# A hybrid SSD, attention and mLSTM step on one core: the rows of decays loaded on SP's queue by the part ahead, an mLSTM tile of their own, one bias buffer

## The chip, the core and the metric

The kernel runs on 1 core of one Trainium2 chip. The metric is the device time of one execution in microseconds (us); lower is better. A core has a matrix engine (TensorE, PE in the profile; PEld is its weight load), VectorE (DVE), ScalarE (ACT), GpSimd (POOL) and SyncE (SP), and 16 DMA engines that move data between the chip's DRAM and the on-chip memory. Each engine runs its own instructions in the order in which they were queued. SP computes nothing here; its queue issues transfers. ScalarE and POOL issue some too, out of the same queue as their computing.

## The reference

One step of one layer of a streaming encoder, for 512 prompt frames and 64 sample frames (T = 576 columns): `x + 1/2 SwiGLU(RMSNorm(x))`, then `+ Mixer(RMSNorm(x))`, then `+ 1/2 SwiGLU(RMSNorm(x))`, and a last RMSNorm. The mixer projects its input once and feeds three branches:

- SSD (Mamba-2): 16 heads of 64 in 4 groups, chunked scan. With `cum = cumsum(dt * a)` the weights inside a chunk are `exp(cum[t] - cum[s])`, and the state enters with `exp(cum)`.
- band attention: 8 heads of 64, with a learned bias on clipped relative distance.
- mLSTM: 4 heads of 128 with exponential gates. With `m` the running maximum of the log weights, a chunk uses `exp(logd - m)` and the state enters with `ei = exp(inter - m)`.

```python
seg = cum[:, :, None] - cum[:, None, :]
lmat = jnp.exp(jnp.where(causal, seg, -jnp.inf))
y = jnp.einsum('btsgr,bsgrp->btgrp', w, xc) + jnp.exp(cum)[..., None] * jnp.einsum('btgn,bgrpn->btgrp', cc, h)
...
s = jnp.einsum('bthd,bshd->btsh', qc, kc) * jnp.exp(logd - mt[:, :, None])
num = jnp.einsum('btsh,bshd->bthd', s, vc) + ei[..., None] * jnp.einsum('bthk,bhkv->bthv', qc, c)
```

Each branch is projected, gated and summed. So the SSD needs, for each of its 16 heads, a row of `cum` over all 576 frames, and the mLSTM, for each of its 4 heads, a row of `-m` and one of `ei`. These are the rows of decays that this case is about.

## The kernel before

All of it is float32, with each operand of a matmul split into a high and a low part (three matmuls a product; the helper at L288 and L289 makes the parts, ScalarE the high one, VectorE the low one). Features lie on the 128 partitions, frames along the free axis. Weights come through rings of buffers: `wr`, `wx` and `wy` for what is loaded, `ph` and `pl` for the parts. SP's queue issues the weight loads (L237, L460, L467), POOL's one accumulating transfer a pair of blocks (L461). The big products (L616) use a scheme of seven products for eight blocks; `uv` (L533) and `g`, `P` (L540, L542) are where ScalarE and VectorE empty their accumulators.

The run has three stages: a first feed-forward part, the mixer, a second feed-forward part. In the mixer the projections are a stream of products. Ahead of every product, `tick` takes one step of a side job (`gates`, until it ends) and one step of the first job in a queue: `attn`, `ml` or `ssd` of one part. The parts come in the order a0 a1 m0 s0 a2 a3 s1 m1 s2 m2 s3 m3, where a is a pair of attention heads, m an mLSTM head and s an SSD group of four heads; an SSD group works in two halves `j` of two heads each. A job yields how many products are to pass until its next step. The program is written in this order, but the order on each engine is set when the kernel is built: the framework places instructions by their place in the program as priority, as soon as its own timing says that operands and buffers are there, and adds the waits. So an instruction with nothing to wait for can be placed far ahead of its part. Tiles of one tag share a number of buffers (`BUFS`), and a new tile waits until an older one of its tag has been read.

`gates` (L784 on) computes all the rows once, at the start of the mixer, from the projection `pre`: it turns `pre` to put frames on partitions (L794), works there, turns the result back, and stores 24 rows of 576 to a scratch tensor in DRAM, `scr_rows` (L839, L853, L856): 0 to 15 the SSD's `cum`, 16 to 19 the mLSTM's `-m`, 20 to 23 its `ei`. `rows` makes an access pattern that reads a row for many partitions, so a load spreads it.

`b` (L176) is the load: it issues, on ScalarE's queue (L181), one transfer of two spread rows, 576 KB, into two of the eight slots of `R1` (128 x 8 x 576, which holds x in the feed-forward parts). It takes slots 2 to 4 and 5 to 7 in turn, whoever calls it. `ml` calls it once at its start and gets `nmB` and `eiB`. `ssd` calls it at its start for both halves, and loads to the third slot of each the same two rows again, 64 partitions each (L1175, 144 KB a transfer). Slots 0 and 1 hold the SSD's gate z.

Readers of the rows. In `ml`: `qt` (POOL, L1045), the tile `D` of decays (VectorE, L1049; `D` is from the ring of four `P` tiles, which attention and the convolution use too), `wc` (ScalarE, L1067) and the state update (VectorE, L1083). In `ssd`, per half: `wd` (VectorE, L1209), `el` (ScalarE, L1212 and L1213), the decay matrices made in place from the first two slots (ScalarE, L1234 to L1237; POOL, L1238), read by matmuls at L1274, and the third slot, made `exp` in place (L1242), multiplied with the state's part (L1282) and added (L1284); the half ends with a product on POOL (L1287) and a store of `ys` on SP (L1288).

`attn` loads the bias table of its two heads at its start on ScalarE's queue (L916), subtracts a constant and masks it on POOL (L918 to L921), and reads it in the prompt's scores (L965) and, last, the sample's (L980, L981). The tag `bias` has two buffers.

Of the kernel before, what the change touches and what calls it, by code (L numbers as in the profile page):

```python
# [31 lines left out]
T = 576  # L32
# [4 lines left out]
NS = 115  # L37
FH = 288
NPLAIN = 4
BUFS = {"g": 9, "t": 5, "P": 4, "Q": 2, "bias": 2}  # L40

FBUFS = {"P": 5, "g": 5, "s": 3}
WBUFS = {"wr": 5, "wx": 4, "wy": 2, "ph": 6, "pl": 6}
# [38 lines left out]
class Hybrid:  # L82
    def __init__(self, ctx, tc, I, O):
        self.tc, self.nc, self.I, self.O = tc, tc.nc, I, O
        self.op = None
        self.stay = {}
        self.plan = []
        self.splan = []
        self.ahead = {}
        self.pin = {}  # L90
        self.b_i = 0
        self.jobs, self.gap, self.side = deque(), 0, iter(())
        nc = self.nc
        self.const = ctx.enter_context(tc.tile_pool(name="const", bufs=1))
        self.dram = ctx.enter_context(tc.tile_pool(name="scr", bufs=1, space=bass.MemoryType.DRAM))
        c = self.const
        self.R1 = c.tile([128, 8, T], F32, name="R1")
        self.rs = c.tile([128, T], F32, name="rs")
        self.small = ctx.enter_context(tc.tile_pool(name="small", bufs=8, reuse_waits="tile"))

        self.wt = ctx.enter_context(tc.tile_pool(name="wt", bufs=1, reuse_waits="tile"))
        self.xs = self.dram.tile([128, 8, T], F32, name="xs")

        self.ys = [self.dram.tile([128, T], F32, name=f"ys{i}") for i in range(16)]
        self.gs = [self.dram.tile([128, T], F32, name=f"gs{i}") for i in range(24)]
        self.scr = self.dram.tile([24, T], F32, name="scr_rows")
# [66 lines left out]
    def unit(self, shape, tag, bufs):  # L173
        return self.fp.tile(list(shape), F32, name=tag, tag=tag, bufs=bufs)

    def b(self, step, r0):  # L176


        i = 2 + self.b_i % 2 * 3
        self.b_i += 1  # L180
        self.nc.scalar.dma_start(self.R1[:, i:i + 2, :], self.rows(r0, 128, step))  # L181
        return [self.R1[:, i + j, :] for j in range(3)]

    def bank(self):
        i = self.bank_i % self.banks
# [598 lines left out]
    def gates(self, pre):  # L784
# [3 lines left out]
        nc, TM = self.nc, self.TM  # L788
        view = lambda i, w: self.R1[:, i, 0:5 * w].rearrange("p (c w) -> p c w", w=w)
        X, u, d, p, q = view(1, 24), view(2, 20), view(3, 20), view(4, 20), view(5, 20)  # L790
        nc.gpsimd.memset(X[64:128, 4, :], 0.0)
        ps = self.ps("x")
        for c, (a, n) in enumerate(CH):
            nc.tensor.transpose(ps[:n, c * 24:(c + 1) * 24], pre[0:24, a:a + n], self.ident[0:24, 0:24])  # L794
# [36 lines left out]
        RT, b, g, M, ei = (self.R1[:, i, :] for i in (6, 2, 3, 4, 5))  # L831
        ps, ps2 = self.ps("x"), self.ps("s")
        for c, (a, n) in enumerate(CH):
            o = ps[:, a:a + n] if c < 4 else ps2[:, 0:n]
# [32 lines left out]
            nc.tensor.transpose(ps[:n, c * 4:c * 4 + 4], b[0:4, a:a + n], self.ident[0:4, 0:4])  # L867
        nc.vector.tensor_copy(TM[:, 0:4, 96:100], ps[:, 0:16].rearrange("p (c w) -> p c w", w=4))
        nc.vector.tensor_copy(TM[:64, 4, 96:100], ps[:64, 16:20])

    def rows(self, r0, n, step=0):

# [159 lines left out]
    def ml(self, h, t):  # L1032
        nc = self.nc
        q, k, v, o = t["q"], t["k"], t["v"], t["o"]
        nmB, eiB, _ = self.b(4, 16 + h)
        C0 = self.unit([128, 130], "c0", 1)
        nc.scalar.dma_start(C0[:, :129], self.I["mc0"][h])
        kt, v1 = self.t("t", (128, 5, 128)), self.t("t", (128, 5, 129))
# [17 lines left out]
        s = self.ps("s")  # L1056
# [15 lines left out]
        for c, (a, n) in enumerate(CH):  # L1072
            if c == 4:
                C = C0
            wv = self.unit([128, 130], "wv", 2)
            nc.scalar.activation(wv[:n, :129], v1[:n, c, :], AF.Copy, scale=wc[:n, c:c + 1])
            pc = self.ps("s")
            nc.tensor.matmul(pc[:, :129], kt[:n, c, :], wv[:n, :129], start=True, stop=True)
            C2 = self.unit([128, 130], "cs", 4)
            if c == 0:  # L1080
                nc.vector.tensor_copy(C2[:, :129], pc[:, :129])
            else:
                nc.vector.scalar_tensor_tensor(C2[:, :129], C[:, :129], eiB[:, a + n - 1:a + n], pc[:, :129],  # L1083
                                               op0=ALU.mult, op1=ALU.add)
            b, o0 = where[c]
            ps = nums[b][:n, o0:o0 + 129]
            nc.tensor.matmul(ps, D[:n, a:a + n], v1[:n, c, :], start=True, stop=(c == 0))
            if c:
                nc.tensor.matmul(ps, qt[:, a:a + n], C[:, :129], start=False, stop=True)
            C = C2  # L1090
            if c >= 3:
                nc.sync.dma_start(self.O["c"][c - 3, h], C[:, :129])
            yield 1
        r = self.unit([128, 8], "r", 2)
        ss = self.unit([128, 8], "ss", 2)
# [2 lines left out]
        for c, (a, n) in enumerate(CH):  # L1098
            b, o0 = where[c]
# [3 lines left out]
        for c, (a, n) in enumerate(CH):  # L1103
            b, o0 = where[c]
# [6 lines left out]
        for c, (a, n) in enumerate(CH):  # L1111
            b, o0 = where[c]
# [55 lines left out]
    def ssd(self, g, t):  # L1168
        nc = self.nc
        Bf, Cf = t["B"], t["C"]  # L1170
        rows = []
        for j in range(2):
            rows.append(self.b(1, 4 * g + 2 * j))
            for r in range(2):
                nc.scalar.dma_start(rows[j][2][r * 64:(r + 1) * 64, :], self.rows(4 * g + 2 * j + r, 64))  # L1175

        last = nc.scalar.activation(self.R1[:, 0, :], self.R1[:, 0, :], AF.Silu)
        with self.tc.issue_after(last.ins):
# [20 lines left out]
        for j in range(2):  # L1199
# [30 lines left out]
            for r in range(2):  # L1230
                e = cum[r]
                tc_ = 32 + d0 + r
                for c, (a, n) in enumerate(CH):
                    nc.scalar.activation(e[:n, a:a + n], e[:n, a:a + n], AF.Relu, scale=-1.0,  # L1234
                                         bias=self.TM[:n, c, tc_:tc_ + 1])
# [10 lines left out]
            for c, (a, n) in enumerate(CH):  # L1246
# [9 lines left out]
                else:  # L1256
                    h = states[c]
# [11 lines left out]
            for c, (a, n) in enumerate(CH):  # L1269
                if c == 4:  # L1270
                    ps = self.ps("s")
                for r in range(2):
                    o = py[r * 64:(r + 1) * 64, a:a + n] if c < 4 else ps[r * 64:(r + 1) * 64, 0:64]
# [13 lines left out]
            nc.gpsimd.tensor_tensor(R[:, 512:], x[:, 515:], R[:, 512:], op=ALU.mult)  # L1287
            nc.sync.dma_start(self.ys[8 + 2 * g + j], R)  # L1288
            yield 1
        yield 3  # L1290

        for j in range(2):
# [316 lines left out]
```

## Time and profile before

| | |
|---|---|
| time, median of 3 runs | 1942.54 us (1939.22 to 1944.31) |
| time of the profiled execution | 1944.79 us |
| its span, first to last instruction | 1943.1 us |
| granted TensorE clock, mean | 0.991 |
| DMA, mean over the span | 152 GB/s |
| rows of 576 KB from `scr_rows`, ScalarE's queue | 12 |
| rows of 144 KB from `scr_rows`, ScalarE's queue | 16 |
| first and last issue of rows | 663.3 and 1145.0 us |

How to read the profile's lines: times are us from the start of the span. A line of a timeline has start, duration, engine, source line, operation, out<-in by tile names, shapes and count; in brackets the idle time of the engine before it and what ended it. An engine with a q is its queue issuing a transfer. A line of waits has who waited, for whom, us in total, times, and the longest. A line of windows has the stretch, then busy us (and instructions) of PE, PEld, DVE, ACT and POOL, then the granted TensorE clock as a share of full speed, the DMA engines' busy share and GB/s. A line of one source line or tile has the durations in ns (least, median, most), then first and last start. A line of DMA issues has tiles, queue, count, KB each and the median us from issue to landing.

### The profile page before, as it was taken

The numbers are of one execution on the slowest core, as the hardware profiler recorded it, in microseconds if no ns is written. First come the engines' busy times: TensorE is split into PE (matmuls) and PEld (weight loads), VectorE is DVE, ScalarE is ACT, GpSimd is POOL, SyncE is SP. The second block draws the span as 40 slices with busy tenths as digits, with TensorE's granted clock in tenths as the row PEclk, the third lists the DMA queues.
The fourth block names the chain that finished last, engine by engine and source line by source line (L and its number), as shares of the span: only waits on it lengthen the run. The fifth ranks groups of instructions, "written<-read, shape, count | busy, mean of one in ns | idle before, by whom it ended". The sixth has DMA issues, their size and how long they took to land. (4 is left out here: it accounts for less than half of the span.)

```text
span 1943.1 us, 37678 instructions
## 1 busy us (share of the span) xinstructions
PE 1887.2 (97%) x13901; PEld 1823.6 (94%) x13901; DVE 1524.6 (78%) x2715; ACT 1089.5 (56%) x2486; POOL 680.1 (35%) x656
## 2 busy tenths in 40 slices
PE   9999999999999999999999998999999999999998
PEld 8899999999999878888888888999999999999998
DVE  8998998988768767667777775745898888988865
ACT  4554654655544777767675765324555455554544
POOL 5343333333202234323435353440233334334311
PEclk9999999999999999899999999999999999999999
DMA  7267666666742545753667557742236666666631
GB/s 241 74 160 173 159 163 163 159 172 163 185 131 80 156 117 159 200 147 108 183 165 183 155 152 213 241 143 88 77 99 165 163 157 172 166 157 167 159 94 60
DMA packets 129440, 294.69 MB, mean 152 GB/s; under 512 B 14289, under 2 KB 26193, under 8 KB 129257
## 3 DMA queue, kind: packets, MB, share of 16 engines
q1 hardware_dynamic: 100072, 205.67, 32.7%
q0 software_dynamic: 19696, 72.10, 20.5%
q10 hardware_dynamic: 9488, 14.53, 2.6%
q8 instruction: 109, 1.79, 0.4%
q14 instruction: 75, 0.61, 0.1%
HBM read 272.87 MB, written 19.38 MB: 150 GB/s over the span
## 5 line engine op out<-in xcount | busy, mean ns | idle before, releaser
L616 PE MATMUL acc<-TH,ph 128*128 128x288 f32 x3220 | 968.0, 301 | 27.4 <-ACT uv L533 11.8
L616 PE MATMUL acc<-TL,ph 128*128 128x288 f32 x3220 | 955.4, 297 | 0.6 <-DVE TL L289 0.6
L616 PE MATMUL acc<-TH,pl 128*128 128x288 f32 x3220 | 955.0, 298 | 1.0 <-DVE pl L289 0.9
L616 PEld LDWEIGHTS acc<-TH,ph 128*128 128x128 f32 x3220 | 607.5, 189 | 46.9 <-ACT uv L533 15.5
L616 PEld LDWEIGHTS acc<-TL,ph 128*128 128x128 f32 x3220 | 609.4, 189 | 4.9 <-issue 3.7
L616 PEld LDWEIGHTS acc<-TH,pl 128*128 128x128 f32 x3220 | 608.4, 189 | 4.8 <-DVE pl L289 2.2
L289 DVE TENSOR_TENSOR pl<-wr,ph 128x512 fp32r<-128x512 f32 x471 | 429.4, 919 | 76.9 <-ACT ph L288 64.5
L288 ACT CAST ph<-wr 128x512 fp32r<-128x512 f32 x471 | 287.9, 620 | 267.9 <-PE acc L616 141.3
L289 DVE TENSOR_TENSOR pl<-wx,ph 128x512 fp32r<-128x512 f32 x390 | 328.1, 845 | 44.5 <-ACT ph L288 37.9
L288 ACT CAST ph<-wx 128x512 fp32r<-128x512 f32 x390 | 237.4, 621 | 201.3 <-POOL wx L472 110.2
L472 POOL TENSOR_TENSOR wx<-wx,wr 128x512 f32<-128x512 f32 x160 | 246.3, 1539 | 188.2 <-DVE pl L289 150.4
L461 POOL DMA_DIRECT2D wx<-in_sblk x115 | 101.6, 901 | 524.1 <-DMA wx<-in_sblk 154.7
L260 PE MATMUL acc<-YH,ph 128*128 128x256 f32 (+1 forms) x768 | 226.5, 298 | 6.3 <-ACT YH L288 5.8
L260 PE MATMUL acc<-YL,ph 128*128 128x320 f32 (+1 forms) x768 | 227.1, 297 | 2.3 <-DVE YL L339 1.9
L260 PE MATMUL acc<-YH,pl 128*128 128x256 f32 (+1 forms) x768 | 226.5, 296 | 0.1
L260 PEld LDWEIGHTS acc<-YH,ph 128*128 128x128 f32 x768 | 145.4, 190 | 6.9 <-ACT YH L288 5.9
L260 PEld LDWEIGHTS acc<-YL,ph 128*128 128x128 f32 x768 | 145.4, 189 | 3.5 <-DVE YL L339 3.3
L260 PEld LDWEIGHTS acc<-YH,pl 128*128 128x128 f32 x768 | 145.2, 189 | 0.3 <-DVE pl L289 0.3
L472 POOL TENSOR_TENSOR wy<-wx,wr 128x512 f32<-128x512 f32 x35 | 56.2, 1605 | 136.0 <-DVE pl L289 120.0
L655 DVE SCALAR_TENSOR_TENSOR R<-acc,R 128x288 f32<-128x288 f32 x168 | 75.7, 450 | 18.6 <-PE acc L616 18.1
L288 ACT CAST TH<-g 128x288 fp32r<-128x288 f32 x120 | 51.6, 434 | 59.8 <-POOL g L641 34.6
L289 DVE TENSOR_TENSOR pl<-wy,ph 128x512 fp32r<-128x512 f32 x70 | 59.8, 857 | 29.6 <-ACT ph L288 26.6
(320 smaller groups left out, 2393.4 us busy)
## 6 DMA issues: line engine op xcount, KB each, us to landing
wr<-in_sblk SPq DMA_DIRECT2D x345, 256.0 KB, 3.6
wx<-in_sblk SPq DMA_DIRECT2D x115, 512.0 KB, 3.8
wx<-in_sblk POOLq DMA_DIRECT2D x115, 512.0 KB, 6.8
wr<-in_wblk SPq DMA_DIRECT2D x126, 256.0 KB, 3.0
R<-scr_rows ACTq DMA_DIRECT2D x12, 576.0 KB, 5.9
gs<-g SPq DMA_DIRECT2D x20, 288.0 KB, 4.5
g<-gs POOLq DMA_DIRECT2D x20, 288.0 KB, 3.9
y<-ys POOLq DMA_DIRECT2D x12, 288.0 KB, 3.8
```

The lines of the kernel that those rows point to most:

```text
L260: nc.tensor.matmul(ps[:, :n], wt[:, wsl], xx[:, k0 + k, a:a + n], start=(k == 0 and i == 0), stop=(k == nk - 1 and i == 2))
L288: self.nc.scalar.copy(hi, src)
L289: self.nc.vector.tensor_tensor(lo, src, hi.bitcast(F32), op=ALU.subtract)
L461: return {"x12": x12, "src": src}, lambda: nc.gpsimd.dma_start(x12, src[:, 1:3, :], accum_op=ALU.add)
L472: add = lambda o, one, two: self.nc.gpsimd.tensor_tensor(o, one, two, op=ALU.add)
L616: self.nc.tensor.matmul(ps, wt[:, wsl], xx[:, kk, :], start=(start and kk == 0 and i == 0), stop=(kk == 3 and i == 2), skip_group_check=True)
L655: self.nc.vector.scalar_tensor_tensor(o, ps, scale, o, op0=ALU.mult, op1=ALU.add)
```

## The change

- `b` and its counter go. `rows_m(h)` loads an mLSTM head's two rows to a tile of their own, tag `rm`, one buffer; `rows_s(g, j)` loads a half of an SSD group, always to slots 2 to 4 for j = 0 and 5 to 7 for j = 1. Both issue on SP's queue and leave the tiles in `self.ahead`, from where `ml` and `ssd` take them.
- Who calls them: the end of `gates` for m0 and both halves of s0; `ml(h)`, after its last state update, for head h + 1; `ssd(g)`, after a half's last step, for the same half of group g + 1.
- The tag `bias` has one buffer instead of two.
- `gates` yields once more at its start, so that the transposes at L794 come with the second product and not with the first.

```diff
--- before.py
+++ after.py
@@ -37,7 +37,7 @@
 NS = 115
 FH = 288
 NPLAIN = 4
-BUFS = {"g": 9, "t": 5, "P": 4, "Q": 2, "bias": 2}
+BUFS = {"g": 9, "t": 5, "P": 4, "Q": 2, "bias": 1}
 
 FBUFS = {"P": 5, "g": 5, "s": 3}
 WBUFS = {"wr": 5, "wx": 4, "wy": 2, "ph": 6, "pl": 6}
@@ -88,7 +88,6 @@
         self.splan = []
         self.ahead = {}
         self.pin = {}
-        self.b_i = 0
         self.jobs, self.gap, self.side = deque(), 0, iter(())
         nc = self.nc
         self.const = ctx.enter_context(tc.tile_pool(name="const", bufs=1))
@@ -173,13 +172,20 @@
     def unit(self, shape, tag, bufs):
         return self.fp.tile(list(shape), F32, name=tag, tag=tag, bufs=bufs)
 
-    def b(self, step, r0):
-
-
-        i = 2 + self.b_i % 2 * 3
-        self.b_i += 1
-        self.nc.scalar.dma_start(self.R1[:, i:i + 2, :], self.rows(r0, 128, step))
-        return [self.R1[:, i + j, :] for j in range(3)]
+    def rows_m(self, h):
+
+        o = self.unit([128, 2, T], "rm", 1)
+        self.nc.sync.dma_start(o, self.rows(16 + h, 128, 4))
+        self.ahead["m", h] = [o[:, j, :] for j in range(2)]
+
+    def rows_s(self, g, j):
+
+
+        nc, i, r0 = self.nc, 2 + 3 * j, 4 * g + 2 * j
+        nc.sync.dma_start(self.R1[:, i:i + 2, :], self.rows(r0, 128, 1))
+        for r in range(2):
+            nc.sync.dma_start(self.R1[r * 64:(r + 1) * 64, i + 2, :], self.rows(r0 + r, 64))
+        self.ahead["s", g, j] = [self.R1[:, i + k, :] for k in range(3)]
 
     def bank(self):
         i = self.bank_i % self.banks
@@ -789,6 +795,7 @@
         view = lambda i, w: self.R1[:, i, 0:5 * w].rearrange("p (c w) -> p c w", w=w)
         X, u, d, p, q = view(1, 24), view(2, 20), view(3, 20), view(4, 20), view(5, 20)
         nc.gpsimd.memset(X[64:128, 4, :], 0.0)
+        yield
         ps = self.ps("x")
         for c, (a, n) in enumerate(CH):
             nc.tensor.transpose(ps[:n, c * 24:(c + 1) * 24], pre[0:24, a:a + n], self.ident[0:24, 0:24])
@@ -867,6 +874,9 @@
             nc.tensor.transpose(ps[:n, c * 4:c * 4 + 4], b[0:4, a:a + n], self.ident[0:4, 0:4])
         nc.vector.tensor_copy(TM[:, 0:4, 96:100], ps[:, 0:16].rearrange("p (c w) -> p c w", w=4))
         nc.vector.tensor_copy(TM[:64, 4, 96:100], ps[:64, 16:20])
+        self.rows_m(0)
+        for j in range(2):
+            self.rows_s(0, j)
 
     def rows(self, r0, n, step=0):
 
@@ -1032,7 +1042,7 @@
     def ml(self, h, t):
         nc = self.nc
         q, k, v, o = t["q"], t["k"], t["v"], t["o"]
-        nmB, eiB, _ = self.b(4, 16 + h)
+        nmB, eiB = self.ahead.pop(("m", h))
         C0 = self.unit([128, 130], "c0", 1)
         nc.scalar.dma_start(C0[:, :129], self.I["mc0"][h])
         kt, v1 = self.t("t", (128, 5, 128)), self.t("t", (128, 5, 129))
@@ -1090,6 +1100,8 @@
             C = C2
             if c >= 3:
                 nc.sync.dma_start(self.O["c"][c - 3, h], C[:, :129])
+            if c == 4 and h < 3:
+                self.rows_m(h + 1)
             yield 1
         r = self.unit([128, 8], "r", 2)
         ss = self.unit([128, 8], "ss", 2)
@@ -1168,11 +1180,7 @@
     def ssd(self, g, t):
         nc = self.nc
         Bf, Cf = t["B"], t["C"]
-        rows = []
-        for j in range(2):
-            rows.append(self.b(1, 4 * g + 2 * j))
-            for r in range(2):
-                nc.scalar.dma_start(rows[j][2][r * 64:(r + 1) * 64, :], self.rows(4 * g + 2 * j + r, 64))
+        rows = [self.ahead.pop(("s", g, j)) for j in range(2)]
 
         last = nc.scalar.activation(self.R1[:, 0, :], self.R1[:, 0, :], AF.Silu)
         with self.tc.issue_after(last.ins):
@@ -1287,6 +1295,8 @@
             nc.gpsimd.tensor_tensor(R[:, 512:], x[:, 515:], R[:, 512:], op=ALU.mult)
             nc.sync.dma_start(self.ys[8 + 2 * g + j], R)
             yield 1
+            if g < 3:
+                self.rows_s(g + 1, j)
         yield 3
 
         for j in range(2):
```

## The prediction

> **What bounds the kernel now.** I read the page first, for the share of each engine, then the waits of TensorE in the mixer's stretch, then the timeline around each longer stop of TensorE, then the waits of the engines that read the rows.
>
> ```profile
> span 1943.1 us, 37678 instructions
> PE 1887.2 (97%) x13901; PEld 1823.6 (94%) x13901; DVE 1524.6 (78%) x2715; ACT 1089.5 (56%) x2486; POOL 680.1 (35%) x656
> ...
> 600.00:1200.00 600.00, 572.52 (x4139) 519.63 (x4138) 432.84 (x907) 413.26 (x1118) 228.15 (x229) 0.98 0.57 154
> ```
>
> TensorE is the bound. In the mixer, roughly from 600 to 1200 us, it is busy for 572.52 of 600 us, so at most 27.5 us of idle time can be taken out there, and whatever a lower granted clock costs beside it. The next view, waits of TensorE in the same stretch, says who ends the idle time.
>
> ```profile
> PE acc L616 <- ACT uv L533: 11.3, 11, 2.9
> PE acc L616 <- DVE g L542: 4.6, 4, 1.6
> PE ps_x L794 <- DVE R L1488: 2.4, 1, 2.4
> ```
>
> TensorE never waits for a row of decays itself. It waits for ScalarE and VectorE to empty the accumulators (uv at L533, g at L542). These two run their instructions in a fixed order, so the question is what they stood still for. The waits of ScalarE and VectorE from 640 to 1200 us name the rows:
>
> ```profile
> ACT el L1212 <- DMA R<-scr_rows: 11.2, 5, 3.1
> ACT R L1242 <- DMA R<-scr_rows: 7.1, 5, 2.4
> ...
> DVE wd L1209 <- DMA R<-scr_rows: 13.1, 6, 4.0
> DVE P L1049 <- DMA R<-scr_rows: 6.3, 3, 2.9
> ```
>
> That is 18.3 us of ScalarE and 19.4 us of VectorE. How much of it reaches TensorE is read from the timeline, each stop of TensorE beside the wait just ahead of it:
>
> ```profile
> 748.20 0.40 PE L616 MATMUL acc<-TH,ph 128*128 128x288 f32 x1 [1.33 <-DVE g L542]
> 791.96 0.40 PE L616 MATMUL acc<-TH,ph 128*128 128x288 f32 x1 [1.59 <-DVE g L542]
> 946.23 0.40 PE L616 MATMUL acc<-TH,ph 128*128 128x288 f32 x1 [0.95 <-ACT uv L533]
> 1045.66 0.40 PE L616 MATMUL acc<-TH,ph 128*128 128x288 f32 x1 [1.49 <-DVE g L542]
> 1099.39 0.40 PE L616 MATMUL acc<-TH,ph 128*128 128x288 f32 x1 [2.87 <-ACT uv L533]
> 1156.66 0.40 PE L616 MATMUL acc<-TH,ph 128*128 128x288 f32 x1 [0.77 <-ACT g L540]
> ```
>
> ```profile
> 746.73 0.17 DVE L1209 TENSOR_TENSOR wd<-R,TM 128x4 f32<-128x4 f32 x1 [3.41 <-DMA R<-scr_rows]
> 790.17 0.49 DVE L1209 TENSOR_TENSOR wd<-R,TM 128x4 f32<-128x4 f32 x1 [3.96 <-DMA R<-scr_rows]
> 944.67 0.69 ACT L1242 ACTIVATE R<-R 128x576 f32<-128x576 f32 x1 [2.03 <-DMA R<-scr_rows]
> 1044.21 1.03 DVE L1049 TENSOR_SCALAR P<-R,TM 128x128 f32<-128x128 f32 x5 [2.36 <-DMA R<-scr_rows]
> 1092.15 0.21 ACT L1212 ACTIVATE el<-R 128x4 f32<-128x4 f32 x1 [2.99 <-DMA R<-scr_rows]
> 1151.57 1.03 DVE L1049 TENSOR_SCALAR P<-R,TM 128x128 f32<-128x128 f32 x5 [2.91 <-DMA R<-scr_rows]
> ```
>
> Each of the six stops comes 1.4 to 7.3 us behind such a wait. Together they are 1.33 + 1.59 + 0.95 + 1.49 + 2.87 + 0.77 = 9.0 us. Two of them have a second price, a lower granted clock right behind (the column ahead of the last two):
>
> ```profile
> 790.00:804.00 14.00, 12.41 (x56) 10.99 (x55) 11.12 (x28) 9.32 (x29) 5.20 (x6) 0.63 0.65 179
> 1090.00:1104.00 14.00, 10.50 (x66) 9.99 (x65) 12.18 (x26) 9.93 (x33) 3.88 (x3) 0.88 0.46 120
> ```
>
> A clock of 0.63 over 14 us is 14 x 0.37 = 5.2 us of matmul time, and 0.88 is 1.7 us. So all that the late rows can cost in this execution is 9.0 + 5.2 + 1.7 = 15.9 us, 0.8% of the time. The Trainium skill, in "TensorE: Matmul & The Clock Gate", Part 1, has the clock halved after an idle window of about 3.4 us; by that alone no stop here would cost any clock, and the sum below would come out 1.7 us higher. The trace does not agree (a stop of 1.59 us stands ahead of the 0.63), and I go by the trace.
>
> **The change part by part.** *Own tile for the mLSTM rows, SSD rows with both slots to themselves.* Before, the twelve loads take slots 2-4 and 5-7 in turn, so the second half of s0 waits for m0 to be done, and the second halves of s2 and s3 for m1 and m2. After, a half of an SSD group has its slots from the same half of the group ahead, and an mLSTM head its tile from the head ahead. The loads go out one part earlier. Whether that removes a wait depends on where the readers stand. These rows tell it:
>
> ```profile
> 674.34 0.38 ACTq L181 DMA_DIRECT2D R<-scr_rows  x1
> ...
> 718.25 1.55 DVE L1049 TENSOR_SCALAR P<-R,TM 128x128 f32<-128x128 f32 x2
> ...
> 909.96 0.61 PE L1189 MATMUL ps_s<-g 128*128 128x128 f32 x4
> ```
>
> The first is m0's load; its reader on VectorE (tile D) comes over 40 us later with no wait for a row, because D stands in the ring of P tiles behind the attention's. So an mLSTM head whose rows come early doesn't wait: the 6.3 us at L1049 go. The SSD rows are different. The wait at 790.17 is for s1's rows, while s1's own first matmul (L1189) is at 909.96: the readers have nothing else to wait for and were put right behind their load, 120 us ahead of need. After the change the same readers can again stand right behind the earlier load, and wait there for its landing.
>
> So I sort the six stops by what is freed when. At 748.20 stands s0's second half behind m0: its rows now come at the start with the first half's, and the stop goes (1.33). At 1099.39 stands s3's second half behind m2: its rows now follow s2's second half some 30 us earlier, and what loads there now is m3, whose reader waits for D (2.87 and the 1.7 of clock go). At 1156.66 stands m3: goes (0.77). At 791.96, s1's rows behind s0's first half, nothing is freed sooner: stays with its 5.2 us of clock. At 946.23 and 1045.66 slots that held an mLSTM head's rows now take an SSD half's: a wait of the same kind stands in the same place, and I leave 0.95 and 1.49 in. Gain: 1.33 + 2.87 + 1.7 + 0.77 = 6.7 us, between 0 (all readers move along with their loads) and 15.9 (all waits go).
>
> *28 issues from ScalarE's queue to SP's.*
>
> ```profile
> L181 ACTq DMA_DIRECT2D R<-scr_rows x12: 332/376/1034, 668.8 to 1145.0; - x12
> L1175 ACTq DMA_DIRECT2D R<-scr_rows x16: 452/458/1113, 663.3 to 1063.6; - x16
> R<-scr_rows ACTq DMA_DIRECT2D x12, 576.0 KB, 5.9
> ...
> ACT ph L288 <- PE acc L616: 92.6, 100, 3.3
> ...
> ACT ph L288 <- DMA wr<-in_sblk: 0.9, 1, 0.9
> ...
> SPq L1288 <- POOL R L1287: 20.9, 7, 5.0
> ```
>
> ScalarE gives up 12 x 0.376 + 16 x 0.458 = 11.8 us of issuing. It is busy for only 413 of 600 us and an issue runs beside the instruction ahead of it, so I take 1 us of gain (between 0 and 11.8). On SP the same 11.8 us stand between weight loads, and SP waits there for the slots to be free. That wait is short: each SSD load follows the store at L1288, which already waits for the POOL instruction behind the last reader of the rows. What is queued behind on SP are the weights; their cover is that the casts wait 92.6 us for TensorE to release a buffer and 0.9 us for a weight to land. I take 0, at most the 11.8. The transfers are the same bytes.
>
> *One bias buffer.* Only the first pair of heads hands over directly to the next:
>
> ```profile
> 679.20 0.24 DVE L981 TENSOR_TENSOR ps_s<-ps_s,bias 64x64 f32<-64x64 f32 x1
> 682.72 0.88 POOL L918 COPY sm<-bias 128x2 f32<-128x2 f32 x1
> 683.70 1.83 POOL L920 TENSOR_SCALAR bias<-bias,sm 128x256 f32<-128x256 f32 x2
> 688.60 0.50 DVE L965 TENSOR_TENSOR ps_s<-ps_s,bias 128x128 f32<-128x128 f32 x2
> bias<-in_bias ACTq DMA_DIRECT2D x4, 256.0 KB, 5.5
> ```
>
> a1's table can now be fetched only after a0's last reader ends at 679.44. With 5.5 us to land and 0.88 + 1.83 us on POOL it is ready near 687.7, against the first reader at 688.60. It just fits: 0, and up to 3 us if POOL or ScalarE stands elsewhere at that moment (nothing below zero, since no reader gets its table sooner).
>
> *The yield in the gates.*
>
> ```profile
> 620.00:630.00 10.00, 7.63 (x45) 6.84 (x44) 10.00 (x19) 3.49 (x7) 2.04 (x3) 0.83 0.16 56
> ```
>
> The transposes at L794 move behind the first product, so the 2.4 us wait need not stand in TensorE's way; with the clock of 0.83 (1.7 us) up to 4.1 us. But VectorE is busy for all 10 of these 10 us with operands that the first products need, so TensorE waits for those next: 0 taken. The gates' results come one product later, before a reader that waits 40 us anyway.
>
> Sum on the profiled execution, 1944.79 us (its span and 1.7 us around it): 1944.79 - 6.7 - 1 = 1937.1. The median of the runs, 1942.54, lies 2.25 us lower; the same difference gives 1934.9, rounded to 1935.
>
> **The rivals.** *All waits go.* If the readers are placed later than their loads, all 15.9 us go, and 1 for ScalarE and up to 1.7 for the start: 1942.5 - 18.6 = 1924. For it: each load has 20 to 100 us more time. Against it: 790.17 shows readers drawn forward to their load. It also needs the slot behind s0's first half to be free sooner, which the change doesn't give.
>
> *Nothing is gained: the loads are earlier but not ahead of their readers.* All six stops find a successor, and only the issuing moves: 1942.5 - 1 = 1941.5. For it: the readers of eight of the twelve loads can follow the load anywhere, and on SP's queue a landing can take longer than the 5.9 us above. The Trainium skill says the like in "DMA: Bandwidth & Descriptors", Issuing engines are not separate DMA queues: starting transfers from another engine saves only its sequencer's time, since all run on the same 16 DMA engines. Against it: m0's D, and the second halves of s0 and s3.
>
> *Slower: SP's queue as the new bound.* A row load that waits on SP for its slot holds up the weights behind it. If this reaches TensorE at each of the eight SSD halves and three later heads with the mean of today's six stops and their clock, 15.9 / 6 = 2.65 us for half of them and nothing for the rest, it costs 11 x 2.65 / 2 = 14.6 us; less the 7.7 of the forecast, 1942.5 + 6.9 = 1949.4. It decides from the point where casts wait for weights as often as for TensorE; 0.9 against 92.6 us speaks against it, and SP's 20.9 us of waiting at L1288, 5.0 at most, for it.
>
> **How the numbers follow.** Forecast (1931 to 1939, the gain of 7.7 us half as large again or half as large) 0.42; all waits gone 0.20; nothing gained 0.25; slower 0.13. The range 1923 to 1947 leaves out the lower half of the second case and most of the last. The likeliest case's own range is 1931 to 1939. What a measurement can tell from no change is 0.3%, 5.8 us: faster means under 1936.7, slower over 1948.4. Faster: 0.20 + 0.28 of the forecast + 0.02 of no gain = 0.50. Slower: 0.09 of the last case + 0.01 = 0.10. Same: 0.40.
>
> **What would show it.** Right: no wait for rows at L1049, none on VectorE or ScalarE near 746 and 1092; the waits at L1209, L1212 and L1242 down from 31.4 us but not near zero; TensorE's waits for uv at L533 down by about 3 us and no half clock near 1100; the time behind the mixer unchanged. The bias step is wrong if POOL waits for the table at L918 beyond 688 us, the SP step if casts or POOL's adds wait longer for weights. A half clock that appears or goes with no row behind it would make the sum wrong by up to 5 us either way.

## The result, and the profile after

The changed kernel takes **1955.98 us** (median of 4 runs, 1951.45 to 1957.64), the kernel before on the same chip 1940.88 us (1938.98 to 1944.31): ratio **1.0077**, 95% interval 1.006 to 1.0094. It is slower by 15 us, where 1935 us was forecast and the range ended at 1947.

The profiled execution took 1957.64 us, with a mean granted clock of 0.984 where 0.991 stood before. Its page:

```profile
span 1955.9 us, 37668 instructions
...
PE 1891.9 (97%) x13901; PEld 1828.1 (93%) x13901; DVE 1529.0 (78%) x2715; ACT 1085.5 (55%) x2484; POOL 679.4 (35%) x656
```

The mixer's stretch, as a window:

```profile
600.00:1200.00 600.00, 564.50 (x4075) 512.88 (x4074) 429.45 (x894) 406.81 (x1096) 224.03 (x227) 0.97 0.56 151
```

In the same 600 us TensorE is idle for 35.5 us, not 27.5, and gets through 4075 matmuls, not 4139. The waits of ScalarE, of VectorE, of POOL and of TensorE from 640 to 1210 us:

```profile
ACT wc L1077 <- DMA rm<-scr_rows: 9.5, 4, 4.8
...
ACT el L1220 <- DMA R<-scr_rows: 6.2, 3, 2.3
...
ACT R L1250 <- DMA R<-scr_rows: 2.0, 3, 1.2
```

```profile
DVE wd L1217 <- DMA R<-scr_rows: 15.1, 8, 3.4
```

```profile
POOL sm L928 <- DMA bias<-in_bias: 19.6, 3, 8.3
```

```profile
PE acc L622 <- ACT g L546: 14.5, 7, 3.5
PE acc L622 <- ACT uv L539: 3.9, 4, 1.6
PE ps_x L1131 <- DVE Q L1125: 3.8, 1, 3.8
```

The waits for rows have moved more than shrunk. VectorE's for the tile D (L1049, 6.3 us) are gone and those at L1217 have grown (13.1 us before). ScalarE's at `wc` (L1077), the small factors of an mLSTM head, are 9.5 us. Before, the same view has them with

```profile
ACT wc L1067 <- DMA R<-scr_rows: 1.7, 2, 1.5
```

To see where the time went I counted the matmuls of the product line (L616 before, L622 after) in both traces and compared the start of the one with the same number. The difference is +0.8 us at the 3600th (675.8 us before), +10.8 at the 3720th (714.9), +14.6 at the 3960th (760.5), and +13.2 at the 6240th (1195.7), where the mixer ends. So 10 us go in one stretch of 39 us, in which the attention pair a0 hands over to a1, and 4 in the next 46, in the end of a1 and in m0. The first stretch, before and then after, as windows:

```profile
676.00:700.00 24.00, 21.23 (x146) 16.32 (x146) 13.54 (x40) 20.87 (x63) 6.53 (x10) 0.93 0.60 168
696.00:714.00 18.00, 18.00 (x123) 13.00 (x122) 11.23 (x32) 14.50 (x46) 3.30 (x8) 1.00 0.36 80
```

```profile
676.00:700.00 24.00, 19.31 (x137) 16.05 (x137) 10.15 (x36) 21.47 (x74) 6.38 (x9) 0.86 0.61 181
696.00:714.00 18.00, 17.09 (x64) 9.45 (x64) 7.21 (x22) 10.51 (x35) 1.27 (x1) 0.53 0.04 17
```

From 696 to 714 the clock was 0.53 and half as many matmuls ran. The trace has it at 0.5 for 17.1 us on end from 696.6. ScalarE's 74 instructions in the first window, where 63 stood, come from here: the pieces of decay matrices (L1234 before, L1242 after) that begin between 676 and 700 us, as the answers for that one line:

```profile
L1234 ACT ACTIVATE R<-R,TM x10: 355/407/412, 676.8 to 679.4; 128x128 f32<-128x128 f32 x8, 64x64 f32<-64x64 f32 x2
```

```profile
L1242 ACT ACTIVATE R<-R,TM x20: 332/388/417, 681.7 to 694.0; 128x128 f32<-128x128 f32 x16, 64x64 f32<-64x64 f32 x4
```

Before, s0's first half made its ten pieces ahead of the hand-over. Now the rows of both halves are loaded at the start, twenty pieces are made, and they lie in the middle of it. The first half's rows also come later than before: m0's load now stands ahead of theirs on SP's queue (669.94, then 670.45), and VectorE first reads them at 678.66, after waiting for 3.37 us, where it read them at 673.87 after 2.26 us. The timeline of TensorE there:

```profile
688.29 0.78 PE L971 MATMUL ps_s<-g 64*128 64x128 f32 x4 [0.63 <-ACT P L995]
...
690.20 0.61 PE L622 MATMUL acc<-TH,ph 128*128 128x288 f32 x1 [1.14 <-ACT g L546]
...
693.24 0.71 PE L956 MATMUL ps_x<-ident,P 128*128 128x128 f32 x5
...
696.91 1.53 PE L1020 MATMUL ps_v<-Q,t 128*64 128x64 f32 x20 [0.96 <-ACT Q L960]
...
709.72 0.59 PE L622 MATMUL acc<-TH,ph 128*128 128x288 f32 x1
```

From 685 to 697 us TensorE stops four times for ScalarE for over half a microsecond (0.94 at 685.76 beside the three in brackets), 3.7 us in all, and between 693.24 and 709.72 no product runs, only a1's small matmuls, in turn with ScalarE's exponentials. From the 20 matmuls at 696.91 to the product at 709.72 it takes 12.8 us, at half clock. Before, the same matmuls take 7.2 us, at full clock, so the half clock costs 5.6 us here:

```profile
693.49 0.95 PE L1010 MATMUL ps_v<-Q,t 128*64 128x64 f32 x20
...
700.68 0.38 PE L616 MATMUL acc<-TH,ph 128*128 128x288 f32 x1
```

The second stretch has one stop, behind the new wait of ScalarE; timelines of ScalarE and TensorE and a window:

```profile
760.47 1.04 ACT L1077 ACTIVATE wc<-TM,rm 128x1 f32<-128x1 f32 x5 [4.78 <-DMA rm<-scr_rows]
```

```profile
763.11 0.47 PE L1131 MATMUL ps_x<-ident,Q 128*128 128x128 f32 x1 [3.81 <-DVE Q L1125]
```

```profile
756.00:770.00 14.00, 10.19 (x59) 9.31 (x59) 5.21 (x17) 9.51 (x22) 3.53 (x4) 0.76 0.59 137
```

That is m1's `wc`. Its rows now load when m0's last state update is done (752.27), and `wc`, which waits for nothing else, was placed right behind that load, in front of a cast of weights (L294) that VectorE waits for (5.44 us), and TensorE behind VectorE. Later `el` does the like: ScalarE waits for 1.90 us at 965.81, ahead of a stop of TensorE of 3.44 us, and at the second half of s3:

```profile
1075.10 0.21 ACT L1220 ACTIVATE el<-R 128x4 f32<-128x4 f32 x1 [1.93 <-DMA R<-scr_rows]
```

```profile
1080.89 0.40 PE L622 MATMUL acc<-TH,ph 128*128 128x288 f32 x1 [3.48 <-ACT g L546]
```

### The profile page after: what moved, and what is told of

Read it like the earlier page. It is cut to its first block, busy times and chain, and to the rows that moved or that the text cites. A ratio compares the mean times of both kernels' runs of the same rounds, so it can differ in the third digit from the quotient of the medians.

```text
span 1955.9 us, 37668 instructions
## 1 busy us (share of the span) xinstructions
PE 1891.9 (97%) x13901; PEld 1828.1 (93%) x13901; DVE 1529.0 (78%) x2715; ACT 1085.5 (55%) x2484; POOL 679.4 (35%) x656
## 5 line engine op out<-in xcount | busy, mean ns | idle before, releaser
L622 PE MATMUL acc<-TH,ph 128*128 128x288 f32 x3220 | 970.4, 302 | 35.3 <-ACT g L546 14.5
L622 PE MATMUL acc<-TL,ph 128*128 128x288 f32 x3220 | 955.8, 297 | 1.2 <-DVE TL L295 1.1
L622 PE MATMUL acc<-TH,pl 128*128 128x288 f32 x3220 | 955.9, 298 | 0.8 <-DVE pl L295 0.8
L622 PEld LDWEIGHTS acc<-TH,ph 128*128 128x128 f32 x3220 | 607.5, 189 | 59.1 <-ACT g L546 17.2
L622 PEld LDWEIGHTS acc<-TH,pl 128*128 128x128 f32 x3220 | 609.1, 189 | 4.9 <-issue 3.2
L622 PEld LDWEIGHTS acc<-TL,ph 128*128 128x128 f32 x3220 | 609.1, 189 | 3.3 <-DVE TL L295 1.9
L294 ACT CAST ph<-wr 128x512 fp32r<-128x512 f32 x471 | 286.9, 617 | 270.3 <-PE acc L622 148.5
L294 ACT CAST ph<-wx 128x512 fp32r<-128x512 f32 x390 | 236.9, 619 | 199.7 <-POOL wx L478 104.7
L294 ACT CAST TH<-g 128x288 fp32r<-128x288 f32 x120 | 51.5, 433 | 59.1 <-POOL g L647 34.7
```

The lines of the kernel that those rows point to most:

```text
L294: self.nc.scalar.copy(hi, src)
L622: self.nc.tensor.matmul(ps, wt[:, wsl], xx[:, kk, :], start=(start and kk == 0 and i == 0), stop=(kk == 3 and i == 2), skip_group_check=True)
```

## The experiments

My theory was that the readers of the rows do the harm: they have nothing to wait for but the load, so the framework places them right behind it, and an earlier load draws them into a place where ScalarE is wanted. The rivals were the single bias buffer, SP's queue, and the yield. Each "before" below is the kernel before on the same chip. "Held" means that a group of instructions is put, in the order of its engine, behind an instruction of its own part (`issue_after`); nothing else changes, and the work is the same.

### Readers of s0's second half held

```diff
+            kept = lambda i: self.tc.issue_after(i.ins) if g == 0 and j == 1 else nullcontext()
...
+            with kept(gate), kept(own):
...
+                with kept(gate):
```

The first `with` holds `wd` and `el` behind the gate's silu and this group's `cb`, the second the pieces of decays and their exponentials (and one more the third slot's).

> The changed kernel with the readers of the rows of s0's second half alone kept behind their own part (as in e5_held, which held all). Reader theory in its narrow form: the 10 us lost between 675 and 715 us come from this half's work, which the earlier load drew into the hand-over from a0 to a1, so 8 to 12 us of the loss go: 1944 to 1948. Wide form (every reader has its share): 2 to 5 us go, 1951 to 1954.

Measured: 1948.5 us (9 runs), ratio 1.0045 (1.0031 to 1.0059). That is 8.5 us above the kernel before on its chip, where the change stood 15.1 above. The two windows:

```profile
676.00:700.00 24.00, 23.38 (x165) 17.52 (x163) 12.66 (x43) 22.81 (x75) 5.67 (x8) 1.00 0.59 183
696.00:714.00 18.00, 18.00 (x133) 14.66 (x133) 11.91 (x32) 14.39 (x43) 2.08 (x4) 1.00 0.44 103
```

Full clock, and products among a1's matmuls again. The readers of that half are what costs the 10 us of this stretch. Not all that is won here is kept: in the table below this stretch is 13.8 us shorter than in the change, and the end of the mixer comes 7.7 us earlier (+5.5 us to before, where the change has +13.2).

### Its load later: a miss, and the mended one

First I only moved the call, so that the load stands later in the program:

```diff
         self.rows_m(0)
-        for j in range(2):
-            self.rows_s(0, j)
+        self.rows_s(0, 0)
...
+            if c == 4 and h == 0:
+                self.rows_s(0, 1)
```

> The changed kernel with the rows of s0's second half loaded where they came before, at the end of m0 (its call moved from the end of the gates to m0's last state update); no reader is held. Narrow reader theory: as e7, 1944 to 1948, since the readers move away with their load. If holding as such helps (and not the place of the work), the loss stays: 1953 to 1958.

Measured: 1956.25 us (4 runs), ratio 1.0076 (1.0056 to 1.0095), as the change. But SP issues it when it did before, since the slots are free and it has nothing to wait for; SP's timeline:

```profile
670.49 4.05 SPq L185 DMA_DIRECT2D R<-scr_rows  x2
```

So this tells nothing of a later load, only that a call's place in the program doesn't set when it goes. The mended one holds the load on SP's queue behind m0's last store of a state:

```diff
+            if c == 4 and h == 0:
+                with self.tc.issue_after(state.ins):
+                    self.rows_s(0, 1)
```

> The changed kernel with nothing altered but that the load of the second half of s0's rows waits on SP's queue behind m0's last store of a state, so that it can't go at 670. If the load that goes early is what brings s0's pieces into the hand-over of a0 to a1: as with the held readers of that half, 1944 to 1949 us, no 17 us at half clock near 697, fewer than 20 pieces of decays on ScalarE between 676 and 700. If the holding of readers helps by something else and the early load is harmless: 1952 to 1958 us, and the half clock stands. The stop for wc near 760 stays by either.

Measured: 1944.28 us (10 runs), ratio 1.0023 (1.0012 to 1.0034). The load goes at 736.9, and the windows show no idle time at all in the first 24 us:

```profile
736.93 0.46 SPq L185 DMA_DIRECT2D R<-scr_rows  x1
```

```profile
676.00:700.00 24.00, 24.00 (x162) 17.06 (x161) 13.64 (x39) 23.08 (x73) 5.65 (x8) 1.00 0.48 144
696.00:714.00 18.00, 18.00 (x138) 15.59 (x137) 12.23 (x31) 14.22 (x39) 4.45 (x5) 1.00 0.47 118
```

Holding the load does what holding its readers did, and somewhat more. No reader is held here, so the early load is the cause of this loss, by way of its readers. One thing more changes with it: with one load less on SP's queue the first half's rows are read at 675.40, not at 678.66.

### `wc` held, alone and with s0's second half

```diff
+        dexp = nc.scalar.activation(D[:, :512], D[:, :512], AF.Exp)
...
+        with self.tc.issue_after(dexp.ins):
+            for c, (a, n) in enumerate(CH):
+                nc.scalar.activation(wc[:n, c:c + 1], self.TM[:n, c, 64 + h:65 + h], AF.Exp, bias=nmB[:n, a + n - 1:a + n])
```

> The changed kernel with wc of the four mLSTM heads alone kept behind D's exponential. If the heads' own tile costs through wc (ScalarE waits 9.5 us at it, 4.8 of them at 760 us ahead of a stop of TensorE of 4 us with a half clock behind it): 4 to 9 us faster than changed, 1947 to 1952, and the 10 us between 675 and 715 stay. If wc's waits cost nothing: within 3 us of changed.

Measured: 1940.12 us (10 runs, 1937.66 to 1948.87), ratio 1.0008 (0.9993 to 1.0022). In the median that is the whole loss, more than the 4 us that the second stretch has, and more than was expected. The hold also takes m0's `wc` out of the hand-over (676.74 in the change, 734.92 here). The profile, taken in the slowest of the ten, still has half clock for 17.1 us near 698. Set against the change, which has it too, the mixer ends 8.1 us earlier (+5.1 us to before, where the change has +13.2). So I ran the same program once more, to see whether the half clock belongs to the program or to the execution:

> The same program as the one that holds only wc (1940.12 us in the median of ten, 1937.66 to 1948.87, its profile taken in the slowest). If the half clock of 17 us near 698 belongs to the program, it stands in this profile too, whatever the time. If it comes and goes between executions, an execution near 1940 shows none there and its product 3720 stands some 8 to 10 us earlier than in the slow one; an execution near 1948 shows it again.

Measured: 1948.48 us, clock 0.984. The windows:

```profile
676.00:700.00 24.00, 19.45 (x132) 15.99 (x131) 10.16 (x35) 20.11 (x67) 5.85 (x9) 0.80 0.57 176
696.00:714.00 18.00, 18.00 (x69) 10.06 (x68) 6.80 (x21) 9.99 (x33) 1.27 (x1) 0.50 0.06 23
```

The half clock is there again, 23.9 us of it from 690.3, with a time near the slowest. Eight of the other nine executions took 1937.66 to 1944.11 us at clocks of 0.988 to 0.991, one 1946.74 at 0.986. The same program thus comes out some 11 us apart, and the time goes with the clock. That the quicker executions lack this half clock fits their times, but none of them was profiled, so it is argued and not shown.

Both held:

> The changed kernel with two groups of readers kept behind their own part: those of s0's second half (as e7_s0_second_held) and wc of the mLSTM heads (as e8_wc_held). Reader theory, with the two losses apart from each other: both go, 1936 to 1944. If e8_wc_held won its time only by a half clock near 696 that comes in some executions: 1942 to 1950, not better than e7_s0_second_held by more than 5 us.

Measured: 1938.19 us (10 runs), ratio 0.9991 (0.9982 to 1.0001). Nothing of the loss is left, with SP's queue, the own tile, one bias buffer and the yield all in place. In the profiles either hold alone leaves the end of the mixer late (+5.5 and +5.1 us), and both together bring it ahead of before (-5.7). In the medians, each set against before on its chip, the hold on s0's half wins 6.6 us, the one on `wc` 15.0, and both 17.0. So the two losses overlap, and s0's half costs less once `wc` is held.

The differences to before by product number, as above, for the change and all kernels made from it, in the profiled execution of each (us gained or lost within the stretch), with the wait of m1's `wc` for its rows:

| kernel | 3600 to 3720 (676 to 715 us) | 3720 to 3960 (715 to 760) | wait of m1's wc | 3960 to 6240 (760 to 1196) |
|---|---|---|---|---|
| the change | +10.0 | +3.8 | 4.8 | -1.4 |
| s0's second half held | -3.7 | +5.2 | 5.3 | +3.3 |
| its load late | -4.6 | +6.5 | 4.6 | -0.6 |
| its call moved (the miss) | +8.2 | -2.5 | 1.7 | +3.2 |
| wc held | +10.9 | -3.1 | none | -4.9 |
| wc held, again | +11.2 | -3.1 | none | -5.2 |
| both held | -2.5 | -3.1 | none | -1.1 |
| two bias buffers (below) | +10.7 | -0.6 | 3.0 | +9.6 |
| ScalarE's queue (below) | +10.3 | -1.5 | 2.6 | +2.5 |
| all readers held (below) | -2.4 | -1.1 | none | -4.0 |

The first column goes with s0's second half: 8 to 11 us lost wherever its readers come early, 2 to 5 won wherever they don't. The second goes with the length of the wait of `wc`: lost from 4.6 us on, won from 3.0 down. How far single executions differ is told by two kernels below: before with one bias buffer, as fast as before, has -1.5, +1.1 and -2.1 in these columns, and before with the yield +0.8, -0.2 and -3.5. So the small numbers of the second column and most of the third say little. The second is not the wait of `wc` alone either: the kernel before with all readers held (below) loses 2.9 us there without any wait for a row.

### All readers of rows held, after and before

Here the readers on VectorE and ScalarE are held in every group and head: D and `wc` behind their head's own steps, `wd`, `el` and the decays behind their group's. This is the changed kernel with these holds:

> The changed kernel, with the readers of the rows kept behind an instruction of their own part on the same engine: in an SSD group, ScalarE's behind the gate's Silu and VectorE's behind the masking of cb; in an mLSTM head, D behind the second turn to frames and wc behind D's exponential. Reader theory: the waits for rows on ScalarE and VectorE (17.7 and 15.1 us) fall under 3 us each, and the time falls by 6 to 10 us, to 1946 to 1950. Table theory: the waits go as well, but the stretch from 675 to 715 us stays, and the time falls by no more than 4 us. Queue theory: no change.

Measured: 1938.04 us (10 runs), ratio 0.998 (0.9969 to 0.9991), lower than any theory expected. No engine waits for a row any more. The kernel before with them:

> The kernel before with the same holds on the readers, loads still on ScalarE's queue. Reader theory: the waits for rows (20.0 us on ScalarE, 19.4 on VectorE) fall under 4 us each, six stops of TensorE and two half clocks go, and it is 5 to 15 us faster than before. If the readers' work is then late for its own part instead, it is no faster or slower, and TensorE waits inside the SSD parts (L1274, L1281).

Measured: 1935.43 us (7 runs, 1933.93 to 1936.44), ratio **0.9974** (0.9963 to 0.9984). This beats both kernels, with the loads where they were before. The mixer's window:

```profile
600.00:1200.00 600.00, 576.44 (x4204) 527.20 (x4203) 430.81 (x919) 419.47 (x1128) 237.31 (x237) 0.98 0.59 158
```

No wait for a row is left here either. The mixer ends 9.4 us earlier in the profile, of the 15.9 that the prediction had as the most; the medians differ by 5.4 us. So no earlier load was needed to be rid of the waits: the readers had to stand later. With the same holds the changed kernel is no faster (1938.04 against 1935.43 us, on the same chip).

Since a hold wins 5.4 us where nothing was loaded early, not all that a hold wins back in the changed kernel need be a loss that the change brought. For s0's second half the late load, which holds no reader, is free of this doubt. For `wc` there is no such run.

### The bias buffer

```diff
-BUFS = {"g": 9, "t": 5, "P": 4, "Q": 2, "bias": 2}
+BUFS = {"g": 9, "t": 5, "P": 4, "Q": 2, "bias": 1}
```

> The kernel before with one bias buffer instead of two, nothing else. Table theory (POOL waits for a1's bias table, and the sums of weights queued behind it on POOL come late, so that TensorE runs out of products between a0 and a1): slower than before by 6 to 11 us, with POOL waiting 5 us or more at the copy out of the bias table and a long half clock near 700 us. Reader theory (the loss comes from the row loads and what stands right behind them) and queue theory (SP's queue): no change, within 3 us.

Measured, as the only edit to before: 1940.23 us (10 runs), ratio 0.9996 (0.9984 to 1.0009). POOL waits for the table, and no engine waits for POOL's work on it:

```profile
POOL sm L918 <- DMA bias<-in_bias: 19.0, 3, 12.2
```

The reverse, two buffers in the changed kernel, needs room, so I took it from `cs` (4 to 3 buffers), `junk` (2 to 1), `st` (7 to 6) and `wv` (2 to 1):

> The changed kernel with two bias buffers; to make room, four small rings lose one buffer each (cs 4 to 3, junk 2 to 1, st 7 to 6, wv 2 to 1). Table theory: 6 to 11 us faster than the changed kernel, so 1945 to 1950, and TensorE's stretch from 675 to 715 us as in the kernel before. Reader and queue theories: as slow as the changed kernel, 1953 to 1958. If the smaller rings cost something of their own, it adds 0 to 4 us to each.

Measured: 1965.35 us (4 runs), ratio 1.0131 (1.0106 to 1.0156). POOL waits for no table any more, and the 10 us at 675 to 715 stay; the rest is the smaller rings or the order that came with them, which this run doesn't separate.

### The queue

```diff
-        self.nc.sync.dma_start(o, self.rows(16 + h, 128, 4))
+        self.nc.scalar.dma_start(o, self.rows(16 + h, 128, 4))
```

(and so the two lines of `rows_s`).

> The changed kernel with its row loads issued on ScalarE's queue instead of SP's; all else as changed. Reader theory (the readers stand right behind the earlier loads, and crowd ScalarE while a0 hands over to a1): the loss stays, 1950 to 1960. Queue theory (row loads on SP's queue hold up the weights): back to 1938 to 1945.

Measured: 1960.39 us (4 runs), ratio 1.0095 (1.0075 to 1.0115). Taking SP's queue back doesn't help the changed kernel. Putting it into the kernel before, in the old slots:

```diff
-        self.nc.scalar.dma_start(self.R1[:, i:i + 2, :], self.rows(r0, 128, step))
+        self.nc.sync.dma_start(self.R1[:, i:i + 2, :], self.rows(r0, 128, step))
```

> The kernel before with its row loads issued on SP's queue instead of ScalarE's, at the same places and in the same slots. Queue theory: slower by 5 to 15 us, weights late behind loads that wait for their slot. Reader theory: within 5 us of before, since the second half of s0 still has to wait for m0's slots.

Measured: 1952.31 us (4 runs), ratio 1.0064 (1.0049 to 1.0079). The waits for rows at `el` and `wd` grow (11.2 and 13.1 us before):

```profile
ACT el L1212 <- DMA R<-scr_rows: 17.0, 7, 4.3
```

```profile
DVE wd L1209 <- DMA R<-scr_rows: 16.9, 7, 3.2
```

The loss is of the size that was expected of late weights, but no cast on ScalarE in the mixer (640 to 1210 us) waits for a weight, so it isn't the weights behind the rows that are late. Of the 8.7 us by which this profiled span is longer, 6.0 come between 760 and 1196 us, at stops such as 3.15 us of TensorE at 943.77, 1.5 us behind a wait of ScalarE for a row. Why the rows are waited for longer this run doesn't settle: the median landing of the 576 KB rows is 6.0 us, where 5.9 stood before.

### The own tile alone, and the yield alone

```diff
-        nmB, eiB, _ = self.b(4, 16 + h)
+        rm = self.unit([128, 2, T], "rm", 1)
+        nc.scalar.dma_start(rm, self.rows(16 + h, 128, 4))
+        nmB, eiB = [rm[:, j, :] for j in range(2)]
```

> The kernel before with one bias buffer (no change by e1_bias_one) and a tile of its own for the mLSTM rows, loads still at the start of each part on ScalarE's queue, no yield. Reader theory: the freed slots alone let the second half of s0 go at the start, its 10 decay pieces stand with the first half's on ScalarE between 676 and 700 us, a half clock of 17 us follows near 696, and the kernel is 7 to 15 us slower than before, most of the change's loss. If the loss needs loads placed in the part ahead or SP's queue: within 4 us of before.

Measured (before with this and one bias buffer): 1959.27 us (4 runs), ratio 1.0098 (1.0079 to 1.0116). The tile by itself frees slots 5 to 7, and s0's second half goes at the start. `wc` waits here too, m1's for 4.6 us:

```profile
ACT wc L1069 <- DMA rm<-scr_rows: 12.2, 4, 4.6
```

Its profile was taken in the fastest of its four executions, 1954.8 us. There the pieces of s0's second half lie in the hand-over as well, and from 694.22 to 704.84 no product runs, but the clock is full from 696 to 714:

```profile
696.00:714.00 18.00, 17.37 (x116) 11.31 (x115) 10.88 (x30) 14.50 (x45) 2.38 (x3) 1.00 0.17 55
```

Only 4.0 us are lost between the 3600th and the 3720th product, and the half clock that was expected isn't there. So some 4 us are the price of the other order, and 5.6 of the rest in the change are the half clock's, by the stretch of a1's matmuls above.

> The kernel before with the one more yield in the gates and nothing else. All theories: within 4 us of before; TensorE's wait of 2.4 us for the gates' projection (L794 before) goes and VectorE, busy throughout that stretch, keeps TensorE waiting nearly as long for the products' operands.

Measured, the yield alone in before: 1944.08 us (10 runs), ratio 1.0018 (1.0009 to 1.0028). Its profiled span, 1939.8, is shorter than before's 1943.1, so its profile can't say where the median's 4 us are; I leave that open.

By themselves the own tile (with one bias buffer) costs 19 us, SP's queue 12, the yield 4 and the bias buffer nothing, and all together 15. They don't add up: each makes another order of instructions.

## Why the prediction was wrong

**What bounds the kernel** was right: TensorE, held up by ScalarE and VectorE that stand still for rows, with at most 15.9 us to win. The kernel before with all readers held won 9.4 in the mixer of its profile, and 5.4 in the median.

**The step that failed** is the sorting of the six stops by "what is freed when", with its gain of 6.7 us: each of the three stops that it took out has a successor. It said of s0's second half: "its rows now come at the start with the first half's, and the stop goes (1.33)". The wait for these rows did shrink, from 3.41 to 0.23 us. But the prediction had itself written that such readers "were put right behind their load, 120 us ahead of need", and then priced only the wait, not the place to which the readers go. Ten pieces, their exponentials and `wd` and `el` went to ScalarE in the hand-over of a0 to a1, and cost 10 us in place of winning 1.33.

Of s3's second half it said that its rows come "some 30 us earlier", and that "2.87 and the 1.7 of clock go". The load is issued 16.3 us earlier (1069.36, 1085.69 before), the readers move along, and the stop of 3.48 us at 1080.89 that is shown above has 3.4 us of half clock right behind it, from 1082.3. Of m3 it said that 0.77 goes with the wait for D. That wait went, and `wc` waits there for 1.98 us instead (1109.50), with a stop of TensorE of 1.15 us at 1111.59. This is the rival "nothing is gained" ("All six stops find a successor"), which priced the successors like the old stops. The bound "0 (all readers move along with their loads)" was false for the same reason: moving along can cost.

**Left out**: `wc`. "So an mLSTM head whose rows come early doesn't wait: the 6.3 us at L1049 go." They went, D being held by its ring, but `wc` reads the same rows and nothing holds it; it waits 9.5 us, and one of these waits stops TensorE for 3.81 us. Before, it waited for 1.7 us, the least of the rows' readers on these two engines. Held alone, it won back the whole loss in the median, so by the medians this gap weighs more than s0's second half.

**SP's queue**, taken at 0 and at most 11.8, measured 12.2 us on its own (1952.31 against 1940.11 of the kernel before on that chip). In the changed kernel it is not the cause, since taking it back made nothing faster. The slower rival (weights behind SP) had the right sign, but neither the size (1949.4 us, measured 1955.98) nor the mechanism: no cast on ScalarE waits for a weight in the mixer, in the change or in the kernel before with SP's queue.

**The bias buffer** at 0 was right, though the step that led there was not: POOL did wait past 688 us, to 689.52. One buffer costs nothing by itself; in the changed kernel VectorE waits once for POOL's work on the table, for 0.9 us. **The yield** at 0 was right to within the 4 us that its run leaves unexplained. **The clock** was named as a danger of "up to 5 us either way". Half of all time at half clock is 19.5 us before and 31.6 after, a difference of 12.1 beside the 12.8 us between the two spans. But this sum is no measure of a loss: in before with all readers held it is 23.3 us, in a span 10.1 us shorter than before's. In the hand-over the half clock has some 6 of the 10 us, by the stretch of a1's matmuls, and the order the rest.

**What it said would show it**: the waits for D are gone, those at `wd`, `el` and the third slot stand at 23.3 us (31.4 before), "down but not near zero", and the time behind the mixer is unchanged (+13.2 us at its end, +12.8 in the span). The half clock near 1100 didn't go; it stands at 1082.3. TensorE's waits for `uv` fell from 10.9 to 3.9 us (640 to 1210 us in both), more than forecast, but those for `g` at ScalarE's L546 came in their place, 14.5 us where 2.1 stood (L540).

What stays open is what sets off the half clock in the hand-over. Stops and a stretch without products stand at it in each profile that has it, and in the one of the own tile they stand there without it. Nor does TensorE's busy time just ahead decide it alone: in the last 3.41 us before the 17.1 us TensorE was busy for 2.09 us in the change. With `wc` held it was 2.05 just ahead, but only 1.87 in the 3.41 us before those, and full clock followed them. None of the quicker executions with `wc` held was profiled.

## What to carry to other kernels

An earlier load isn't an earlier result alone: where a framework places instructions as soon as their operands are there, every reader of the load moves with it, so look at each reader, ask what else it waits for, and price the place to which it goes. Where waits for a load are the trouble, hold the readers later before you load earlier; here that won 0.26% with no other change, and the change without it lost 0.77%. Judge a reordering by the granted clock too: here 3.7 us of short stops stood ahead of a stretch that lost 5.6 us to the clock.

## What the runs showed of the hardware

In the changed kernel no stop of TensorE between 685 and 714 us is longer than 1.14 us, and yet the clock stood at half for 17.1 us. The Trainium skill, in "TensorE: Matmul & The Clock Gate", Part 1, gives an idle window of about 3.4 us as what halves it. By single idle times the trace doesn't agree. The stretches at half clock do last 3.4, 6.8, 10.2, 13.7, 17.1 and 23.9 us in these traces, whole multiples of that window, but for the last of each, which ends with the execution. In each of the sixteen traces they all start on one grid of 3.41 us (134 starts, none over 5 ns off it).

In the kernel before, moving 28 issues from ScalarE's queue to SP's cost 0.64%. The same skill, in "DMA: Bandwidth & Descriptors", Issuing engines are not separate DMA queues, says that the issuer saves only its sequencer's time. The landing of the 576 KB rows agrees (6.0 against 5.9 us), but the kernel's time didn't follow from it.
